# The second matmul of a score tile, 64 or 128 rows deep

## The chip, the cores and the metric

One core of a Trainium2 chip runs the whole program. The metric is the device time of one execution in microseconds; the time given is the median of three runs. The engines are named as the profile names them: PE (matmul; PEld is its weight load), DVE, ACT, POOL and SP, whose queue starts the DMAs.

## The reference

The program is an encoder trunk of two layers over 1024 tokens of width 1024, all in float32. Layer 0 mixes tokens by differential attention: 8 heads, each with two score maps of head dimension 64, a distance penalty and a softmax over all keys. Layer 1 mixes by a windowed attention of 16 heads of dimension 64 on a 16 x 64 grid. Both are followed by a gated feed-forward part (hidden width 2816) and a gated embedding that is added.

```python
s = jnp.einsum("mbhqd,mbhkd->mbhqk", qblk, k).astype(jnp.float32) * scale + bias
a = jax.nn.softmax(s, axis=-1)
a = a[0] - lam * a[1]
...
s = jnp.einsum('bhqd,bhkd->bhqk', qr, kb).astype(jnp.float32) + bias
s = jnp.where(key_mask, s, -jnp.inf)
a = jax.nn.softmax(s, axis=-1)
```

## The kernel before

Every float32 matrix is split into a high and a low part, and a product is made of the parts' products. For a score tile (128 queries x 512 keys in layer 0, x 384 or 256 in layer 1) the head dimension is only 64, so the query's two parts are stacked into one tile of 128 rows, `qs`: for map (or head) m = 0 the high part in rows 0 to 63 and the low part in rows 64 to 127, for m = 1 the other way round. The key's high part is stored twice, `kh`, in both halves of the rows: one 128-row product (L193) gives high x high plus low x high. The key's low part, `kl`, is stored once, m = 0 in the upper rows and m = 1 in the lower: a second product of 64 rows (L196) gives high x low. Both accumulate into one bank of PSUM, `s`.

`qk` makes these tiles for one head (layer 0) or one pair of heads (layer 1): per operand and half 24 products (L131) into a tile `d`, then ACT writes the high parts, DVE subtracts to get the low parts (L170, L173), and POOL copies the high part of the key to the other half (L185).

In layer 0, `attend` goes over eight blocks of 128 queries. For a block it scores 4 tiles (two maps, two halves of the keys), DVE adds the distance penalty and takes the running maximum (L273), ACT takes exponentials (L281), POOL scales one map and DVE subtracts the other (L298, L300), PE transposes the result (L306, 8 products a block), ACT and DVE split it into parts `at` (L89, L92), and 24 products with the values for each two blocks (L312) and a norm follow. Score tiles have three banks, exponentials four buffers, two a block. In heads 0 to 3 (`PAIRED`) the two maps of a key half are issued together, in the others one tile after another. In layer 1 the same steps run over 16 blocks (two heads of a pair, eight column blocks): score, bias and maximum (L421), exponential (L425), scaling on POOL (L428), transpose (L432), split, products with the values (L407).

While one head attends, PE also does the projections of the next heads: 96 products of `qk` (L131) for each head and 192 of `values` (L209) for each two heads, at the last head the first part of the output projection (L495). The program is written head after head; a scheduler puts it in order at build time, and each engine then follows its own fixed list. The projections are what it mixes between score tiles. How far ahead they can be placed depends on free buffers: `qs`, `kh` and `kl` have two each, the value tiles `v` four (`% 4`), each 8 KB a partition.

Of the kernel before, what the change touches and what calls it, by code (L numbers as in the profile page):

```python
# [12 lines left out]
F32 = mybir.dt.float32  # L13
F32R = mybir.dt.float32r
F16 = mybir.dt.float16
AF = mybir.ActivationFunctionType
ALU = mybir.AluOpType
# [3 lines left out]
P = 128  # L21
D = 1024
S = 1024
NT = S // P
# [17 lines left out]
MASKED = -1e30  # L42
RING = 5
EARLY = 5
# heads whose two maps are scored together, so that their 64-row products share the array
PAIRED = 4
EXP_LN_SET = 6
# the three products that carry a float32 product: (stationary part, moving part)
PASSES = ((0, 0), (0, 1), (1, 0))


class Trunk:
# [21 lines left out]
        self.hs = self.dram.tile([NT, P, D], F32, name="hs")  # L74
        self.hp = self.dram.tile([NT, P, D], F32, name="hp")

# [1 line left out]
    def open_hn(self):  # L78
        self.hnpool = self.tc.alloc_tile_pool(name=self.nc.get_next_instruction_name(), bufs=1, side="right",
                                              reuse_waits="tile")  # L80
# [58 lines left out]
                    self.nc.tensor.matmul(ps[:, c], lhs(i, k), rhs(j, k, c),  # L139
                                          start=k == 0 and n == 0, stop=k == nk - 1 and n == 2)  # L140

# [1 line left out]
    def qk(self, u, pools, bias=None, q_scale=1.0):  # L143
        nc = self.nc
        qkp, psd = pools["qk"], pools["d"]
        qs = qkp.tile([P, 2, S], F32R, tag=f"qs{u % 2}", name="qs")
        kh = qkp.tile([P, 2, S], F32R, tag=f"kh{u % 2}", name="kh")
        kl = qkp.tile([P, S], F32R, tag=f"kl{u % 2}", name="kl")
        top, bot = slice(0, 64), slice(64, 128)
        for which in range(2):  # L150
            w = self.weights(pools["wqk"][2 * u + which], self.slab, "slab")
            b = None if bias is None else bias[:, which * 8 + u:which * 8 + u + 1]
            for half in range(2):
                c = slice(half * HALF, (half + 1) * HALF)
                ps = psd.tile([P, HALF], F32, tag="d", name="d")
                self.mm_feat(ps, w, half)

                sc = q_scale if which == 0 else 1.0

                def hi(out, rows):  # L160
                    if b is None and sc == 1.0:
                        nc.scalar.copy(out=out, in_=ps[rows])
                    elif b is None:
                        nc.scalar.activation(out=out, in_=ps[rows], func=AF.Copy, scale=sc)
                    else:
                        nc.scalar.activation(out=out, in_=ps[rows], func=AF.Identity, bias=b[rows], scale=1.0)

                def lo(out, rows, h):
                    if b is None:
                        nc.vector.scalar_tensor_tensor(out=out, in0=ps[rows], scalar=sc, in1=h.bitcast(F32),  # L170
                                                       op0=ALU.mult, op1=ALU.subtract)
                    else:
                        nc.vector.scalar_tensor_tensor(out=out, in0=ps[rows], scalar=b[rows], in1=h.bitcast(F32),  # L173
                                                       op0=ALU.add, op1=ALU.subtract)

                if which == 0:
                    hi(qs[top, 0, c], top)
                    hi(qs[bot, 1, c], bot)
                    lo(qs[bot, 0, c], top, qs[top, 0, c])
                    lo(qs[top, 1, c], bot, qs[bot, 1, c])  # L180
                else:
                    hi(kh[top, 0, c], top)
                    hi(kh[bot, 1, c], bot)
                    for m, (to, src) in enumerate(((bot, top), (top, bot))):
                        nc.gpsimd.tensor_scalar(out=kh[to, m, c], in0=kh[src, m, c].bitcast(F32), scalar1=1.0,  # L185
                                                scalar2=0.0, op0=ALU.mult, op1=ALU.add)
                    lo(kl[top, c], top, kh[top, 0, c])
                    lo(kl[bot, c], bot, kh[bot, 1, c])
        return qs, kh, kl

    def score_part(self, part, s, qs, kh, kl, m, qc, kc):
        if part == 0:
            self.nc.tensor.matmul(s, qs[:, m, qc], kh[:, m, kc], start=True, stop=False)  # L193
        else:
            b = slice(64 * m, 64 * m + 64)
            self.nc.tensor.matmul(s, qs[b, m, qc], kl[b, kc], start=False, stop=True)  # L196

    def scores(self, *args):
        for part in range(2):
# [11 lines left out]
                                          start=k == 0 and n == 0, stop=k == KT - 1 and n == 2)  # L211
            sink(t, ps)

# [1 line left out]
    def diff_attention(self, first):  # L215
        nc, tc, a = self.nc, self.tc, self.a
        with ExitStack() as st:
            pool = lambda name, bufs, **k: st.enter_context(tc.tile_pool(name=name, bufs=bufs, reuse_waits="tile", **k))
            pools = {"qk": pool("da_qk", 1), "wqk": a["da_qk"]}
            vp = pool("da_v", 1)  # L220
# [24 lines left out]
            vt = {}  # L245

            def values(p2, psd):
                for j in range(2):
                    vt[2 * p2 + j] = vp.tile([P, NT, 2, P], F32R, tag=f"v{(2 * p2 + j) % 4}", name="v")

                def sink(t, ps):
                    for j in range(2):
                        v = vt[2 * p2 + j]
                        self.split((v[:, t, 0], v[:, t, 1]), ps[:, j * P:(j + 1) * P], nc.scalar)
                self.v_units(p2, a["da_v"], psd, sink, first if p2 == 0 else None)

            def attend(h, ops):
                qs, kh, kl = ops
                v = vt[h]
                otile = self.ob.tile([P, 2, CB, P], F32R, tag="ot", name="ot")  # L260
                ot = otile.rearrange("p l b (r c) -> p l b r c", c=8)
                for ch in range(4):
                    at = atp.tile([P, 2, NT, 256], F32R, tag="at", name="at")
                    for i in (2 * ch, 2 * ch + 1):
# [13 lines left out]
                        def exponent(m):  # L278
# [3 lines left out]
                                                 scale=SLOPES[h], accum_out=sm[:, m:m + 1])  # L282

                        qc = slice(i * P, (i + 1) * P)
                        order = (((0, 0), (1, 0)), ((0, 1), (1, 1))) if h < PAIRED else \
                            (((0, 0),), ((0, 1),), ((1, 0),), ((1, 1),))
                        for group in order:
                            ps = [ps_s.tile([P, HALF], F32, tag="s", name="s") for _ in group]
                            for part in range(2):
                                for (m, half), s in zip(group, ps):  # L290
                                    self.score_part(part, s, qs, kh, kl, m, qc, slice(half * HALF, (half + 1) * HALF))
                            for (m, half), s in zip(group, ps):
                                biased_max(m, half, s)
                                if half == 1:
                                    exponent(m)
# [55 lines left out]
                    ops = project(h + 1)  # L351
            self.out_proj_first(0, a["da_wo"], psd)

# [1 line left out]
    def neighborhood_attention(self):  # L355
        nc, tc, a = self.nc, self.tc, self.a
        with ExitStack() as st:
# [13 lines left out]

            def values(p4, psd):
                for j in range(2):
                    vt[2 * p4 + j] = vp.tile([P, NT, 2, 2, 64], F32R, tag=f"v{(2 * p4 + j) % 4}", name="v")

                def sink(t, ps):
                    for j in range(2):
                        v = vt[2 * p4 + j]
                        src = ps[:, j * P:(j + 1) * P].rearrange("p (m d) -> p m d", m=2)
                        self.split((v[:, t, :, 0], v[:, t, :, 1]), src, nc.scalar)  # L380
                self.v_units(p4, a["na_v"], psd, sink)
# [79 lines left out]
                    ops = self.qk(u + 1, pools, bq)  # L461
            self.out_proj_first(1, a["na_wo"], psd)

# [1 line left out]
    def keep(self, layer, u, ot):  # L465
        if u == PAIRS - 1:
            self.last = ot
# [171 lines left out]
        self.close_hn()  # L639


# [1 line left out]
def _units(w, n, width):  # L643
    k = w.shape[0]
    return w.reshape(k // P, P, n, width).transpose(2, 1, 0, 3)
# [64 lines left out]
```

## Time and profile before

| what | us |
|---|---|
| median of 3 runs (lowest, highest) | 3075.58 (3072.76, 3077.97) |
| span of the profiled execution | 3072.8 |
| PE busy | 3025.0 (98%) |
| PEld busy | 2410.6 (78%) |
| DVE busy | 1524.7 (50%) |
| ACT busy | 783.0 (25%) |
| POOL busy | 625.2 (20%) |

The profiled execution's time is the span, which is that of the fastest of the three runs to the tenth. Layer 0's attention lies between 71 and 740 us, layer 1's between 1695 and 2160 us of the span. A share over the whole span mixes stages: the feed-forward parts lie between and behind. Products are pipelined, so that the busy time of a product overlaps that of the next; how much time one adds is read from starts or from the chain of work that ended last.

### The profile page before, as it was taken

The numbers are of one execution on the slowest core, as the hardware profiler recorded it, in microseconds if no ns is written. First come the engines' busy times: TensorE is split into PE (matmuls) and PEld (weight loads), VectorE is DVE, ScalarE is ACT, GpSimd is POOL, SyncE is SP. The second block draws the span as 40 slices with busy tenths as digits, with TensorE's granted clock in tenths as the row PEclk, the third lists the DMA queues.
The fourth block names the chain that finished last, engine by engine and source line by source line (L and its number), as shares of the span: only waits on it lengthen the run. The fifth ranks groups of instructions, "written<-read, shape, count | busy, mean of one in ns | idle before, by whom it ended". The sixth has DMA issues, their size and how long they took to land.

```text
span 3072.8 us, 36422 instructions
## 1 busy us (share of the span) xinstructions
PE 3025.0 (98%) x14304; PEld 2410.6 (78%) x14304; DVE 1524.7 (50%) x2793; ACT 783.0 (25%) x1576; POOL 625.2 (20%) x766
## 2 busy tenths in 40 slices
PE   7999999999999999999999999999999999999998
PEld 7777777677788888888888878877778888888886
DVE  5677777775622323333444565666533333322354
ACT  3445454443200000000212444543200000000021
POOL 2232333332200000010112332332210001000121
PEclk9999999999999999999999999999999999999999
DMA  3010101243211111111123121136321111111112
GB/s 132 15 42 28 42 28 35 73 147 113 94 48 48 49 48 48 42 48 54 38 74 102 39 82 54 60 104 203 129 62 48 42 48 49 48 48 49 50 45 78
DMA packets 83866, 198.54 MB, mean 65 GB/s; under 512 B 6768, under 2 KB 39664, under 8 KB 83696
## 3 DMA queue, kind: packets, MB, share of 16 engines
q1 hardware_dynamic: 83696, 196.22, 20.4%
q8 instruction: 113, 1.85, 0.3%
q14 instruction: 57, 0.47, 0.1%
HBM read 164.74 MB, written 31.46 MB: 64 GB/s over the span
## 4 chain that ended last, share of the span: by engine, by line
PE 96%; DVE 2%; DMA 1%; issue 1%; ACT 0%; POOL 0%; POOLq 0%; SPq 0%; DVEq 0%; ACTq 0%
PE mm L131 32%; PE mm L139 17%; PE d L131 12%; PE d L209 7%; PE mm L599 6%; PE s L196 5%; PE d L495 3%; PE av L312 3%; PE s L193 3%; PE tr L306 2%; PE mm L595 1%; PE o L407 1%; PE tr L124 1%; PE tr L432 1%; DMA st<-da_wo 0%
## 5 line engine op out<-in xcount | busy, mean ns | idle before, releaser
L131 PE MATMUL mm<-hnT,w 128*128 128x512 f32 x4224 | 997.9, 397 | 2.5 <-DVE h L518 1.5
L131 PEld LDWEIGHTS mm<-hnT,w 128*128 128x128 f32 x4224 | 796.1, 189 | 197.5 <-POOL rs L113 1.7
L91 POOL TENSOR_SCALAR w<-st 128x1024 fp32r<-128x1024 f32 (+1 forms) x248 | 256.1, 1034 | 1619.2 <-PE mm L131 794.4
L92 DVE TENSOR_TENSOR w<-st,w 128x1024 fp32r<-128x1024 f32 (+1 forms) x248 | 282.8, 1142 | 490.1 <-POOL w L91 489.7
L139 PE MATMUL mm<-w,act 128*128 128x512 f32 x2112 | 486.0, 390 | 0.9 <-DVE h L552 0.9
L139 PEld LDWEIGHTS mm<-w,act 128*128 128x128 f32 x2112 | 395.7, 188 | 83.9 <-DVE h L552 1.7
L131 PE MATMUL d<-hnT,w 128*128 128x512 f32 x1536 | 405.0, 407 | 0.0
L131 PEld LDWEIGHTS d<-hnT,w 128*128 128x128 f32 x1536 | 280.1, 189 | 80.6 <-issue 22.2
L552 DVE TENSOR_TENSOR h<-h,mm 128x1024 f32<-128x1024 f32 x176 | 213.6, 1218 | 153.6 <-PE mm L139 153.2
L541 ACT ACTIVATE sil<-mm 128x1024 f32<-128x1024 f32 x44 | 45.4, 1031 | 791.4 <-PE mm L131 791.4
L542 DVE TENSOR_TENSOR sil<-sil,mm 128x1024 f32<-128x1024 f32 x44 | 53.7, 1221 | 374.1 <-PE mm L131 374.1
L209 PE MATMUL d<-w,hnT 128*128 128x256 f32 x1536 | 236.4, 295 | 1.6 <-POOL w L91 1.1
L209 PEld LDWEIGHTS d<-w,hnT 128*128 128x128 f32 x1536 | 201.2, 191 | 26.2 <-issue 21.8
L92 DVE TENSOR_TENSOR at<-tr,at 128x512 fp32r<-128x512 f32 (+2 forms) x288 | 157.4, 552 | 69.3 <-ACT at L89 56.0
L599 PE MATMUL mm<-w,hnT 128*128 128x512 f32 x768 | 188.4, 397 | 0.0
L281 ACT ACTIVATE e<-e,mx 128x1024 f32<-128x1024 f32 x128 | 147.2, 1150 | 130.9 <-DVE mx L279 126.1
L89 ACT CAST at<-tr 128x512 fp32r<-128x512 f32 (+2 forms) x288 | 133.6, 483 | 167.6 <-PE tr L432 106.2
L196 PE MATMUL s<-kl,qs 64*128 64x512 f32 (+2 forms) x384 | 175.5, 473 | 0.0
L89 ACT CAST act<-sil 128x1024 fp32r<-128x1024 f32 x44 | 46.4, 1054 | 489.6 <-DVE sil L542 489.6
L599 PEld LDWEIGHTS mm<-w,hnT 128*128 128x128 f32 x768 | 143.1, 188 | 33.5
L193 PE MATMUL s<-kh,qs 128*128 128x512 f32 (+2 forms) x384 | 156.7, 414 | 7.3 <-DVE kl L170 3.1
L196 PEld LDWEIGHTS s<-kl,qs 64*128 64x128 f32 x384 | 68.2, 183 | 93.5 <-issue 91.0
(101 smaller groups left out, 3003.0 us busy)
## 6 DMA issues: line engine op xcount, KB each, us to landing
st<-gu SPq DMA_DIRECT2D x88, 512.0 KB, 3.6
st<-wd SPq DMA_DIRECT2D x44, 512.0 KB, 3.5
ot<-ot SPq DMA_DIRECT2D x28, 512.0 KB, 3.9
o<-ot SPq DMA_DIRECT2D x16, 640.0 KB, 4.7
st<-da_qk SPq DMA_DIRECT2D x16, 512.0 KB, 3.6
hp<-r SPq DMA_DIRECT2D x16, 512.0 KB, 4.7
r<-hp SPq DMA_DIRECT2D x16, 512.0 KB, 3.5
st<-wpg SPq DMA_DIRECT2D x16, 512.0 KB, 3.6
```

Of the source, the lines that this page charges most:

```text
L89: hi_engine.copy(out=w[0], in_=src)
L91: hi_engine.tensor_scalar(out=w[0], in0=src, scalar1=1.0, scalar2=0.0, op0=ALU.mult, op1=ALU.add)
L92: self.nc.vector.tensor_tensor(out=w[1], in0=src, in1=w[0].bitcast(F32), op=ALU.subtract)
L131: self.nc.tensor.matmul(ps, w[:, i, kt * P:(kt + 1) * P], self.hnT[half][:, j, kt, :], start=kt == 0 and n == 0, stop=kt == KT - 1 and n == 2)
L139: self.nc.tensor.matmul(ps[:, c], lhs(i, k), rhs(j, k, c), start=k == 0 and n == 0, stop=k == nk - 1 and n == 2)
L193: self.nc.tensor.matmul(s, qs[:, m, qc], kh[:, m, kc], start=True, stop=False)
L196: self.nc.tensor.matmul(s, qs[b, m, qc], kl[b, kc], start=False, stop=True)
L209: self.nc.tensor.matmul(ps, self.hnT[t // 4][:, i, k, c], ws[k // 4][:, j, (k % 4) * 256:(k % 4 + 1) * 256], start=k == 0 and n == 0, stop ...
L281: nc.scalar.activation(out=e[m], in_=e[m], func=AF.Exp, bias=mx[:, m:m + 1], scale=SLOPES[h], accum_out=sm[:, m:m + 1])
L312: nc.tensor.matmul(av, v[:, kb, x], at[:, y, kb, :], start=kb == 0 and n == 0, stop=kb == NT - 1 and n == 2)
L552: nc.vector.tensor_tensor(out=h[t], in0=h[t], in1=acc, op=ALU.add)
L599: nc.tensor.matmul(acc[:, 0], self.hnT[t // 4][:, i, k, cs], ws[k // 2][:, j, k % 2], start=k == 0 and n == 0, stop=k == KT - 1 and n == 2)
```

## The change

The key's low part becomes a tile of the same shape as the high part. DVE writes it to the same rows as before, one plane for each m, and POOL copies each plane to the other half of the rows, as it does with the high part. The second product then takes all 128 rows of the stacked query and of the doubled low part; it adds low x low, which was left out before. The order of the score tiles is now one for all heads: the two key halves of a map together. Value tiles have three buffers in place of four.

```diff
-        kl = qkp.tile([P, S], F32R, tag=f"kl{u % 2}", name="kl")
+        kl = qkp.tile([P, 2, S], F32R, tag=f"kl{u % 2}", name="kl")
...
                     hi(kh[top, 0, c], top)
                     hi(kh[bot, 1, c], bot)
-                    for m, (to, src) in enumerate(((bot, top), (top, bot))):
-                        nc.gpsimd.tensor_scalar(out=kh[to, m, c], in0=kh[src, m, c].bitcast(F32), scalar1=1.0,
-                                                scalar2=0.0, op0=ALU.mult, op1=ALU.add)
-                    lo(kl[top, c], top, kh[top, 0, c])
-                    lo(kl[bot, c], bot, kh[bot, 1, c])
+                    lo(kl[top, 0, c], top, kh[top, 0, c])
+                    lo(kl[bot, 1, c], bot, kh[bot, 1, c])
+                    for x in (kh, kl):
+                        for m, (to, src) in enumerate(((bot, top), (top, bot))):
+                            nc.gpsimd.tensor_scalar(out=x[to, m, c], in0=x[src, m, c].bitcast(F32), scalar1=1.0,
+                                                    scalar2=0.0, op0=ALU.mult, op1=ALU.add)
...
     def score_part(self, part, s, qs, kh, kl, m, qc, kc):
-        if part == 0:
-            self.nc.tensor.matmul(s, qs[:, m, qc], kh[:, m, kc], start=True, stop=False)
-        else:
-            b = slice(64 * m, 64 * m + 64)
-            self.nc.tensor.matmul(s, qs[b, m, qc], kl[b, kc], start=False, stop=True)
+        self.nc.tensor.matmul(s, qs[:, m, qc], (kh, kl)[part][:, m, kc], start=part == 0, stop=part == 1)
...
-                    vt[2 * p2 + j] = vp.tile([P, NT, 2, P], F32R, tag=f"v{(2 * p2 + j) % 4}", name="v")
+                    vt[2 * p2 + j] = vp.tile([P, NT, 2, P], F32R, tag=f"v{(2 * p2 + j) % 3}", name="v")
...
-                        order = (((0, 0), (1, 0)), ((0, 1), (1, 1))) if h < PAIRED else \
-                            (((0, 0),), ((0, 1),), ((1, 0),), ((1, 1),))
-                        for group in order:
+                        for group in (((0, 0), (0, 1)), ((1, 0), (1, 1))):
...
-                    vt[2 * p4 + j] = vp.tile([P, NT, 2, 2, 64], F32R, tag=f"v{(2 * p4 + j) % 4}", name="v")
+                    vt[2 * p4 + j] = vp.tile([P, NT, 2, 2, 64], F32R, tag=f"v{(2 * p4 + j) % 3}", name="v")
```

On PE, in the middle of head 0 of layer 0, the order before has products of the next values (`d<-w,hnT`) between all score tiles:

```order
L209 MATMUL d<-w,hnT_96 128x256 x10
L193 MATMUL s<-kh,qs 128x512
L196 MATMUL s<-kl,qs 128x512
L209 MATMUL d<-w,hnT_96 128x256 x8
L312 MATMUL av<-at,v 128x256
L209 MATMUL d<-w,hnT_96 128x256
L193 MATMUL s<-kh,qs 128x512
L196 MATMUL s<-kl,qs 128x512
L209 MATMUL d<-w,hnT_96 128x256 x4
```

In the changed kernel the last of these stand in the middle of head 0, and score tiles, transposes (`tr`) and value products (`av`) follow alone (L191 is both products of a tile, L204 was L209, L299 was L306, L305 was L312):

```order
L204 MATMUL d<-w,hnT_95 128x256 x7
L191 MATMUL s<-kh,qs 128x512
L191 MATMUL s<-kl,qs 128x512
L299 MATMUL tr<-ident,e 128x128 x8
L191 MATMUL s<-kh,qs 128x512
L191 MATMUL s<-kl,qs 128x512
L191 MATMUL s<-kh,qs 128x512
L191 MATMUL s<-kl,qs 128x512
L191 MATMUL s<-kh,qs 128x512
L191 MATMUL s<-kl,qs 128x512
L305 MATMUL av<-at,v 128x256
```

The next product of a projection comes 23 tiles after the one at the top, 13 tiles into head 1: most value products of the next pair have moved from the first head into the second.

On PE, where head 2 of layer 0 begins in the changed kernel, the projection of its keys (L129, was L131) ends right ahead of its first score tile:

```order
L129 MATMUL d<-hnT_96,w 128x512
L299 MATMUL tr<-ident,e 128x128 x8
L312 MATMUL msp<-sq,ones 128x256
L129 MATMUL d<-hnT_96,w 128x512 x23
L191 MATMUL s<-kh,qs 128x512
L191 MATMUL s<-kl,qs 128x512
L305 MATMUL av<-at,v 128x256
L129 MATMUL d<-hnT_95,w 128x512 x2
L305 MATMUL av<-at,v 128x256 x23
L129 MATMUL d<-hnT_95,w 128x512 x4
L191 MATMUL s<-kh,qs 128x512 x2
L191 MATMUL s<-kl,qs 128x512
```

Before, the last product of that projection stood 18 rows ahead of the head's first score tile.

## Rows read from the trace of the kernel before

**Rows 1.** Windows: us, then busy us (instructions) per engine, granted clock, DMA.

```profile
core 0: us, PE busy (x) PEld busy (x) DVE busy (x) ACT busy (x) POOL busy (x), PEclk, DMA share, GB/s
...
149.20:234.70 85.50, 85.50 (x456) 64.89 (x454) 66.27 (x154) 41.70 (x87) 31.36 (x35) 1.00 0.12 38
...
1695.00:2092.00 397.00, 391.11 (x2092) 313.22 (x2091) 246.40 (x735) 187.43 (x486) 131.77 (x179) 1.00 0.24 74
```

**Rows 2.** The chain: start us, us it adds, what; plain products and transposes.

```profile
424.98 0.87 PE tr L306 x8
...
1672.77 22.49 PE d L131 x96
```

**Rows 3.** The chain around one score tile, and a run of value products.

```profile
228.83 0.23 PE s L193
229.06 0.42 PE s L196
229.49 1.84 PE d L131 x7
231.32 2.74 PE av L312 x23
```

**Rows 4.** Timeline of PE in head 0: start us, us, what.

```profile
117.02 0.50 PE L196 MATMUL s<-kl,qs 64*128 64x512 f32 x2
```

**Rows 5.** Timeline of PE in layer 1, two tiles running.

```profile
1795.27 0.44 PE L193 MATMUL s<-kh,qs 128*128 128x384 f32 x1
1795.64 0.44 PE L196 MATMUL s<-kl,qs 64*128 64x384 f32 x1
1796.01 4.24 PE L131 MATMUL d<-hnT,w 128*128 128x512 f32 x17
```

**Rows 6.** Groups of DVE, 71 to 740 us: busy us, mean ns, idle before.

```profile
L273 DVE CUSTOM_DVE_ANT_0 e<-s,strip,mx 128x512 f32<-128x512 f32 x128 | 95.1, 745 | 43.0 <-PE s L196 42.2
L273 DVE CUSTOM_DVE_ANT_0 e<-s,strip 128x512 f32<-128x512 f32 x128 | 87.5, 685 | 37.2 <-PE s L196 23.5 <-PE tr L306 12.4
L92 DVE TENSOR_TENSOR at<-tr,at 128x512 fp32r<-128x512 f32 x128 | 86.6, 684 | 10.4 <-ACT at L89 10.2
L300 DVE SCALAR_TENSOR_TENSOR e<-e,rc 128x1024 f32<-128x1024 f32 x64 | 85.4, 1335 | 11.8 <-POOL e L298 11.5
...
L273 DVE DVE_READ_ACCUMULATOR2_ANT mx<- 128x1 f32 x256 | 20.9, 82 | 0.0
...
L279 DVE TENSOR_SCALAR mx<-mx 128x1 f32<-128x1 f32 x128 | 18.3, 145 | 0.5
L330 DVE SCALAR_TENSOR_TENSOR o<-o,sub,y 128x256 f32<-128x256 f32 x30 | 18.1, 602 | 1.9 <-POOL y L329 1.8
L297 DVE TENSOR_TENSOR rc<-rc,neglam 128x1 f32<-128x1 f32 x64 | 16.0, 250 | 1.0
L92 DVE TENSOR_TENSOR ot<-o,ot 128x256 fp32r<-128x256 f32 x30 | 14.0, 466 | 0.7 <-ACT ot L89 0.4
...
L323 DVE TENSOR_SCALAR sq<-msp 128x256 f32<-128x256 f32 x31 | 13.0, 420 | 12.4 <-PE msp L319 12.2
...
L296 DVE RECIPROCAL rc<-sm 128x2 f32<-128x2 f32 x64 | 10.3, 161 | 18.9 <-ACT e L281 18.7
```

**Rows 7.** Windows around the late weights of the output projection, layer 0.

```profile
595.00:605.00 10.00, 7.53 (x31) 5.46 (x30) 6.38 (x14) 3.84 (x7) 4.85 (x4) 0.83 0.58 159
...
608.00:624.00 16.00, 13.18 (x56) 8.52 (x55) 15.55 (x33) 6.43 (x13) 6.47 (x7) 0.93 0.65 188
```

**Rows 8.** Groups of DVE, 1695 to 2092 us.

```profile
L421 DVE CUSTOM_DVE_ANT_0 s<-s,bias 128x384 f32<-128x384 f32 x84 | 47.1, 563 | 27.1 <-PE s L196 26.3
...
L92 DVE TENSOR_TENSOR at<-tr,at 128x384 fp32r<-128x384 f32 x55 | 30.2, 552 | 16.5 <-ACT at L89 16.1
...
L448 DVE SCALAR_TENSOR_TENSOR of<-o,bq,tmp 64x1024 f32<-64x1024 f32 x13 | 16.7, 1282 | 3.3 <-ACT tmp L447 3.1
...
L421 DVE DVE_READ_ACCUMULATOR2_ANT mx<- 128x1 f32 x112 | 15.2, 136 | 0.2
...
L92 DVE TENSOR_TENSOR ot<-of,ot 128x1024 fp32r<-128x1024 f32 x6 | 7.4, 1226 | 0.0
```

**Rows 9.** Copies of the key's high part, whole span.

```profile
L185 POOL TENSOR_SCALAR kh<-kh 64x512 fp32r<-64x512 f32 x64 | 51.5, 804 | 48.8 <-ACT kh L162 24.1 <-issue 10.6 <-ACT kh L166 9.5
```

More of the change, by code (lines that the diff above doesn't have):

```diff
@@ L44 @@
 EARLY = 5
-PAIRED = 4
 EXP_LN_SET = 6
```

## The prediction

> **What bounds the kernel now.** First the windows, one for the second head of layer 0 and one for nearly all of layer 1: PE has no gap in the first (85.50 of 85.50 us) and next to none in the second (391 of 397), while DVE works 66.27 us (0.78) and 246 us [rows 1]. Both attention layers are bound by PE, with DVE second and, in layer 0, not far behind. A busy PE may still stream little, so the next view is the chain in order of time, which counts only what each product adds: a run of 96 ordinary 512-column products takes 22.49 us, 0.234 us each [rows 2].
>
> In the chain around one score tile the full-depth product (L193) adds 0.23 us, the 64-row one (L196) 0.42, and the run of seven L131 behind it takes 1.84 us, where seven at 0.234 are 1.64 [rows 3]. So a 64-row product costs 0.19 us more than a full one of as many columns, and the product behind it another 0.20: **0.385 us a tile** over two plain products.
>
> **What the change removes.** All 384 second products become 128-row ones, priced at 0.234 us each since L131 has the same form [rows 2]. Layer 0 has 256 tiles. Where two 64-row products with different halves stand side by side they start within one piece of 0.50 us, x2 [rows 4]: there the second is free. This happens at 12 places in the whole trace, all in heads 0 to 3, so 24 tiles gain only 0.385 - 0.234 = 0.15 us a pair. Layer 0: 232 x 0.385 + 12 x 0.15 = 91 us. In layer 1 consecutive starts of L193, L196 and the next product are 0.37 us apart, 0.74 a tile [rows 5]; two plain 384-column products would be 2 x 0.234 x 384/512 = 0.35, so 0.385 again, and 128 tiles give 49 us. Together 140 us, if PE stays the only limit.
>
> A rule that speaks against the change: the Trainium skill, TensorEngine Tiling (Array Packing), Theoretical Speedup, says that products of at most 64 rows can run two at a time, up to twice as fast. The pair of [rows 4] agrees; if every tile had been so paired, layer 0 would gain 128 x 0.15 = 19 us, not 91. What is left here goes by the 12 places.
>
> **What it moves.** The low part of the key doubles in size, and the value tiles go from four buffers to three. A head pair then can't have both next value tiles while its first head still reads one. The order shows the consequence. Before, no more than five tiles stand between two pieces of projection work. Now the first head of a pair gets 96 projection products and 48 of the values', and then there is nothing to mix in until that head's last product with its values is done: 23, 26 and 25 tiles in a row in layer 0 (the last ten or so of heads 0, 2, 4 and the first half of the head behind), three times 12 in layer 1, with only their own transposes and value products.
>
> In such a stretch a block of 128 queries (4 tiles) needs of PE: 8 products x 0.234 = 1.9; 8 transposes 0.9 (0.87 in the chain [rows 2]); 12 value products at 2.74/23 = 0.12, 1.4 [rows 3]; 0.1 for the norm: 4.35 us. Of DVE it needs, from [rows 6]: four biased maxima 4 x 0.715 and their four readouts 0.33; the small ones 0.29, 0.16, 0.25; the combination 1.335; two splits of 0.684; half of 0.42 + 0.60 + 0.47, once in two blocks. That is 7.34 us. **DVE becomes the limit there.**
>
> How much of a stretch DVE can fill is not shown for a stretch like this. From 608 to 624 us, the place where weights of the output projection come late and PE works 13.18 us, it was 15.55 of 16, 0.97 [rows 7]; with PE never short it is 0.78 [rows 1]. I take 0.92, nearer to the first, where PE has gaps as here, and keep 0.85 and 0.97 as bounds.
>
> Layer 0: 74 tiles are 18.5 blocks, DVE 136 us, at 0.92 148 us, where PE needs 80: 68 us lost. The other stretches with few products a tile (16 tiles in head 0 beside 96 projection products; 21 tiles in head 5 beside 144 of values) come close to DVE too; 21 tiles are 38.5 us of DVE at 1.835 us each, 42 at 0.92, where PE needs 38. I put 13 us on all of these, an estimate, 0 to 20. Against it, DVE may still be behind when the next fill begins, and work that off later: three score banks are in flight, so some 3 us at each of three ends, -10.
>
> Layer 1: 12 tiles need of DVE 12 x (0.53 + 0.14 + 0.15 + 0.16) (0.56 for the wide tiles, less for the quarter with 256 columns), then 30 transposed blocks at 0.2 and 1.5 times 1.28 + 0.61 at the ends [rows 6, 8]: 20.8 us. PE needs 12 x 0.33 + 30 x 0.11 + 24 x 0.14 (value products by their widths) = 10.7. A tile passes five engines in turn here, so I take 0.90: 23.1 us, three times 12.4 us lost, less 1 us each of lag: 34.
>
> **The added copies.** POOL copies the low part as it copies the high one: 64 more, 0.80 us each in the mean [rows 9], 51 us. They wait for DVE's low part, so in POOL's queue whatever is behind them waits too: the next softmax scaling or weight split, by a microsecond or so. PE feels them where a second head of a pair ends: the last projection product now stands right ahead of the next head's first score, with 24 value products and 6 of the next projection, 4.3 us, as cover ahead of the second half of the keys. Four copies are 3.2 us, and the high part must first be made and the low part subtracted. Cover gone, 3.2 us at each head would be the price; I take 2 us at three heads of layer 0 and 1 us at three of layer 1: 6 and 3 us. DMAs and weights are as before.
>
> **The sum.** Layer 0: 91 - 68 - 13 + 10 - 6 = 14 us won. Layer 1: 49 - 34 - 3 = 12 us won. 3072.8 - 26 = 3046.8 for the profiled execution. Its span equals the lowest of three runs, with nothing shown around it; the median of the runs is 2.8 us higher, so **3049 us**. DVE's share alone gives 3036 us at 0.97 and 3065 at 0.85.
>
> **Rivals.**
> *The lag hides most of the stretches (faster).* If DVE holds 0.97 and carries a whole block (7.3 us) of lag over each end, layer 0 loses 140 - 80 - 22 + 3 = 41, layer 1 64 - 32 - 5 = 27: 91 + 49 - 68 = 72 us won, 3004 us. For it: in the order, 192 projection products come in the odd heads with only 19 or 11 tiles among them, room to catch up. Against it: only three score banks and two blocks' exponentials are held.
>
> *The clock falls in the stretches (slower).* PE would idle four tenths of each. In the windows with such idling the granted clock was 0.83 and 0.93 [rows 7]: part of each at 1.2 GHz, with PE busy 7.53 us of 10 and 13.18 of 16. At the low level a block costs PE 8.7 us, more than DVE's 8.0. If most of the stretches ran so, at 9.5 us a block: 18.5 x 1.5 = 28 us more in layer 0; in layer 1 21.4 us of PE in a chain with DVE, some 3 us each, 9; and some 10 for runs of fill that begin slow. 3049 + 47 = 3096 us. It turns the result to slower once about six tenths of the stretches run low. Against it: a slow PE idles less, so it may come back. The Trainium skill, TensorE: Matmul & The Clock Gate, A second HAM failure mode: psum-queue depth-cycling, tells of just such small idle times between groups that make the clock swing; by it the 3096 would be the time.
>
> *The copies hold up every head (slower).* If POOL's queue delays all 14 later heads by four copies, 14 x 3.2 = 45 us instead of 9: 3085 us. For it: POOL waits in order; against it: in the order only three starts a layer stand right behind the last projection product.
>
> *The change does not do what it says.* If the extra 0.385 us comes from something else than the 64 rows (two products that accumulate in one bank, or that load the same queries), it stays, and only the losses come: PE then needs 5.9 us a block, 148 - 109 = 39 and 3 x 7.7 = 23 us: about 3138. Against it: L131 accumulates in one bank too, at 0.234.
>
> **How the numbers follow.** The forecast with its own range, 3030 to 3068, has 0.50; the lag 0.17; the clock 0.20; the copies 0.08; no gain 0.05. A measurement of this kernel can tell about 0.2%, 6 us, from no change: below 3069.4 is faster, above 3081.7 slower. The forecast gives 0.45 to faster and 0.05 to within 0.2%; the lag 0.17 to faster; the clock, weak or strong, 0.03 to faster, 0.05 to within, 0.12 to slower; the copies 0.02 to within and 0.06 to slower; no gain 0.05 to slower. That makes 0.65, 0.12 and 0.23. The range, 3004 to 3093, leaves out the far half of the lag, the full clock case and no gain, some 2 in 10.
>
> **What would show it.** Second products spaced like first ones, and no 0.2 us behind them: 0.234 in the chain. In layer 0, three stretches of about 45 to 52 us in which PE is some 0.6 busy and waits for DVE's maxima, and DVE is 0.9 busy or more. The granted clock of these stretches decides between the forecast and the clock rival; POOL's L186 named by waiting score products, the copies. I am wrong if PE stays full there, or if DVE is well under 0.85 with PE waiting for something else.

## The result, and the profile after

| | median us (lowest, highest) | span of the profiled execution |
|---|---|---|
| before | 3075.66 (3072.76, 3077.97), 4 runs | 3072.8 |
| after | 3003.9 (3000.46, 3005.15), 4 runs | 3001.5 |

The change makes the kernel 72 us faster: 0.9765 of the time before, 95% interval 0.9751 to 0.9779. The forecast was 26 us faster, and its range, from 3004 on, just misses the measured time.

Between the first score of layer 0 and its last norm product lie 625.2 us, 672.5 before: 47 won, where 14 were forecast. Layer 1, from its first score to the first product of the stage behind its attention: 441.2 us against 464.9, 24 won, where 12 were forecast. The rest did not change.

From the page after: span, engines' busy time, and the chain's shares.

```profile
span 3001.5 us, 36482 instructions
...
PE 2917.3 (97%) x14304; PEld 2418.2 (81%) x14304; DVE 1528.3 (51%) x2793; ACT 777.1 (26%) x1576; POOL 668.3 (22%) x830
...
PE 91%; DVE 5%; issue 2%; POOL 1%; DMA 1%; ACT 1%; POOLq 0%; SPq 0%; DVEq 0%; ACTq 0%
```

PE lost 108 us of busy time, but only 71 us of span: it now has gaps. Windows of after (columns as in [rows 1]) show where: the three stretches without other work in layer 0, a window behind the first one with other work in it, two of layer 1's three stretches, and both stages whole.

```profile
120.80:158.90 38.10, 31.34 (x174) 23.29 (x173) 35.17 (x91) 24.25 (x50) 14.74 (x17) 0.96 0.00 1
271.30:312.80 41.50, 34.30 (x186) 24.57 (x185) 39.39 (x105) 26.59 (x54) 15.98 (x18) 0.96 0.00 1
419.80:461.40 41.60, 33.67 (x190) 25.62 (x188) 39.29 (x107) 27.50 (x57) 16.35 (x19) 0.96 0.00 1
...
158.90:184.00 25.10, 25.10 (x188) 23.93 (x187) 22.39 (x63) 15.17 (x36) 7.87 (x9) 1.00 0.14 43
...
1685.00:1703.00 18.00, 14.35 (x81) 10.57 (x79) 14.91 (x59) 13.47 (x39) 6.12 (x11) 1.00 0.08 26
1791.40:1810.10 18.70, 15.32 (x81) 11.90 (x79) 15.07 (x59) 13.54 (x39) 6.13 (x11) 0.91 0.08 25
...
71.60:696.80 625.20, 588.02 (x3344) 497.31 (x3343) 501.95 (x1201) 318.23 (x647) 243.17 (x274) 0.98 0.19 60
1649.00:2090.20 441.20, 424.44 (x2418) 366.99 (x2417) 282.94 (x842) 207.95 (x547) 164.86 (x228) 0.99 0.31 99
```

The stretches stand where the order showed them: 23, 26 and 25 tiles in layer 0, three times 12 in layer 1. PE is 0.80 to 0.83 busy there, DVE 0.92 to 0.95 in layer 0 and 0.81 to 0.83 in layer 1. With other work behind the first of them PE is full again. The stretches are shorter than forecast: 121.1 us in layer 0 (148 forecast), 55.0 in layer 1 (69.3).

The chain of after, where other work is at hand:

```profile
162.98 0.36 PE d L204 x3
163.34 0.46 PE s L191 x2
163.80 0.48 PE d L204 x4
```

A tile's two products take 0.46 us, 0.65 in [rows 3], and the four value projections behind add 0.12 each, like the three ahead: nothing is late behind the second product any more.

### The profile page after: what moved, and what is told of

It reads as the page before. It is cut to its first block, busy times and chain, and to the rows that moved or that the text cites. A ratio compares the mean times of both kernels' runs of the same rounds, so it can differ in the third digit from the quotient of the medians.

```text
span 3001.5 us, 36482 instructions
## 1 busy us (share of the span) xinstructions
PE 2917.3 (97%) x14304; PEld 2418.2 (81%) x14304; DVE 1528.3 (51%) x2793; ACT 777.1 (26%) x1576; POOL 668.3 (22%) x830
## 3 DMA queue, kind: packets, MB, share of 16 engines
q8 instruction: 113, 1.85, 0.3%
## 4 chain that ended last, share of the span: by engine, by line
PE 91%; DVE 5%; issue 2%; POOL 1%; DMA 1%; ACT 1%; POOLq 0%; SPq 0%; DVEq 0%; ACTq 0%
PE mm L129 33%; PE mm L137 18%; PE d L129 12%; PE d L204 6%; PE mm L592 6%; PE s L191 4%; PE d L488 3%; PE av L305 3%; PE mm L588 1%; PE tr L299 1%; PE tr L122 1%; PE o L400 1%; PE tr L425 1%; DVE e L268 1%; DVE at L90 1%
## 5 line engine op out<-in xcount | busy, mean ns | idle before, releaser
L129 PE MATMUL mm<-hnT,w 128*128 128x512 f32 x4224 | 997.7, 397 | 1.6 <-ACT hnT L87 0.5
L129 PEld LDWEIGHTS mm<-hnT,w 128*128 128x128 f32 x4224 | 795.5, 189 | 196.4 <-ACT hnT L87 1.0
L129 PE MATMUL d<-hnT,w 128*128 128x512 f32 x1536 | 386.3, 399 | 0.0
L129 PEld LDWEIGHTS d<-hnT,w 128*128 128x128 f32 x1536 | 286.6, 189 | 64.1
L204 PE MATMUL d<-w,hnT 128*128 128x256 f32 x1536 | 224.0, 290 | 2.0 <-POOL w L89 1.0
L204 PEld LDWEIGHTS d<-w,hnT 128*128 128x128 f32 x1536 | 207.0, 193 | 9.5 <-POOL w L89 1.4
L191 PE MATMUL s<-kh,qs 128*128 128x512 f32 (+2 forms) x384 | 154.2, 410 | 24.8 <-DVE mx L268 13.0
L191 PE MATMUL s<-kl,qs 128*128 128x512 f32 (+2 forms) x384 | 142.9, 379 | 0.0
L488 PE MATMUL d<-w,o 128*128 128x512 f32 x480 | 129.6, 406 | 7.4 <-POOL w L89 4.7
```

Source lines behind the costliest of these rows:

```text
L129: self.nc.tensor.matmul(ps, w[:, i, kt * P:(kt + 1) * P], self.hnT[half][:, j, kt, :], start=kt == 0 and n == 0, stop=kt == KT - 1 and n == 2)
L191: self.nc.tensor.matmul(s, qs[:, m, qc], (kh, kl)[part][:, m, kc], start=part == 0, stop=part == 1)
L204: self.nc.tensor.matmul(ps, self.hnT[t // 4][:, i, k, c], ws[k // 4][:, j, (k % 4) * 256:(k % 4 + 1) * 256], start=k == 0 and n == 0, stop ...
L488: nc.tensor.matmul(acc, o[:, k, i, :], ws[k][:, j, c], start=k == 0 and n == 0, stop=k == EARLY - 1 and n == 2)
```

## The experiments

Two theories were held against each other. **A**: the change takes 0.385 us a tile off PE, 140 us in all, and some 64 of them are given back in stretches where DVE limits, which come from the value buffers alone. **B**: only the 0.19 us in the second product itself was to be had, about 70 us, and the stretches cost nothing. Both give about 3000 to 3004 us for the changed kernel. Ratios are to the kernel before, timed again beside each run (3074.6 to 3075.2 us). e4 and e9 leave out low x low, as the kernel before does and with it e3, e6 and e8, which are made from it; the four whose names end in "twice" do some work again.

**e1_value_parts.** The changed kernel with value tiles in pieces, so that parts of both next tiles find room while the pair's first head still reads its own: halves in seven buffers in layer 0 (the room of 3.5 tiles), quarters in 13 in layer 1 (3.25 tiles). So the room grows too, from 3 tiles; pieces and room were not tried apart.

```diff
-                for j in range(2):
-                    vt[2 * p2 + j] = vp.tile([P, NT, 2, P], F32R, tag=f"v{(2 * p2 + j) % 3}", name="v")
+                for part in range(2):
+                    for j in range(2):
+                        n = 4 * p2 + 2 * part + j
+                        vt[2 * p2 + j, part] = vp.tile([P, NT // 2, 2, P], F32R, tag=f"v{n % 7}", name="v")
...
+                for u in (2 * p4 - 3, 2 * p4 - 2):
+                    free.extend(held.pop(u, []))
+                for part in range(4):
+                    for j in range(2):
+                        n = free.pop(0)
+                        held.setdefault(2 * p4 + j, []).append(n)
+                        vt[2 * p4 + j, part] = vp.tile([P, NT // 4, 2, 2, 64], F32R, tag=f"v{n}", name="v")
```

> The changed kernel with its value tiles cut into parts (halves in layer 0, seven buffers of 4 KB; quarters in layer 1, thirteen of 2 KB), so that three quarters (layer 0) and five eighths (layer 1) of the next pair's values can be made while the first head of a pair still reads its own; nothing else differs. Theory A (each second product of 64 rows cost 0.385 us on PE, 140 us in all, and about 64 us of that went back into the six stretches without other work, where DVE sets the time): the stretches vanish and most of the 64 us come, 3004 - 50 = about 2954 us (2940 to 2970). Rival B (the 72 us are the whole gain on PE, 0.19 us a tile, the excess of the 64-row product alone; what stands behind it in the chain is bookkeeping, and the stretches cost nothing net): 3004 us, within 6.

Measured: 2946.56 us, 0.9585 [0.957, 0.9599], 57 us less than after. Windows of this kernel: its head 1, then both stages.

```profile
139.70:207.70 68.00, 67.81 (x412) 59.69 (x411) 62.70 (x152) 39.63 (x84) 31.18 (x35) 1.00 0.13 40
72.20:656.80 584.60, 570.84 (x3344) 497.49 (x3343) 501.21 (x1201) 313.78 (x647) 250.13 (x274) 0.99 0.21 65
1610.10:2032.40 422.30, 413.12 (x2417) 363.60 (x2416) 280.45 (x842) 207.96 (x545) 164.97 (x228) 1.00 0.31 101
```

PE is full again (67.81 of 68.00), with DVE close behind (62.70). Layer 0 is 40.6 us shorter than after and layer 1 18.9. By B nothing was to be won here. This kernel is the fastest of this study, 128 us under the kernel before.

**e4_rows64.** The changed kernel, copies and buffers and all, but the second product on 64 rows again.

```diff
-        self.nc.tensor.matmul(s, qs[:, m, qc], (kh, kl)[part][:, m, kc], start=part == 0, stop=part == 1)
+        b = slice(64 * m, 64 * m + 64) if part else slice(0, P)
+        self.nc.tensor.matmul(s, qs[b, m, qc], (kh, kl)[part][b, m, kc], start=part == 0, stop=part == 1)
```

> The changed kernel with all its tiles, copies, buffers and order of tiles, but the second product takes 64 rows again (of the doubled low part only the half that was written first is read). A: 384 x 0.385 = 148 us more on PE, of which some 36 us hide in the stretches where DVE sets the time: 3004 + 105 = about 3109 us (3090 to 3125). B: 3004 + 72 = 3076 us.

Measured: 3112.77 us, 1.0125 [1.011, 1.014], 109 us more than after. That is more than B's whole 70, so the price is above 0.19 us a tile. Up to some 20 of the 109, an estimate from the stretches of layer 1 (see e3), go with a lower clock and not with the rows alone; e9 has the price without them.

**e3_before_three_values.** The kernel before with three value buffers.

```diff
-                    vt[2 * p2 + j] = vp.tile([P, NT, 2, P], F32R, tag=f"v{(2 * p2 + j) % 4}", name="v")
+                    vt[2 * p2 + j] = vp.tile([P, NT, 2, P], F32R, tag=f"v{(2 * p2 + j) % 3}", name="v")
```

(The same in layer 1.)

> The kernel before with three value buffers in place of four, and nothing else. A: in the stretches without other work PE then needs 5.9 us a block of queries (4.35 + 4 x 0.385), close to the 6.55 us that DVE gave in the changed kernel, so that little is lost: 18 blocks x 0.7 = 12 us in layer 0, 36 tiles x 0.22 = 8 us in layer 1, 3076 + 20 = 3096 us (3085 to 3110). B: the buffers cost nothing, 3076 us within 6.

Measured: 3114.98 us, 1.013 [1.0113, 1.0147]. The lost buffer alone costs 40 us, and e4 is level with this kernel: low part twice, its copies and the new tile order cost nothing that can be told. It is 19 us above what was expected, most of that in layer 1, which from its first to its last score takes 25 us longer (475 against 450; 8 were expected); layer 0 takes 15.5 longer (12 expected). Windows of a stretch of layer 0 and of two of layer 1:

```profile
125.70:161.50 35.80, 34.14 (x170) 22.42 (x169) 32.57 (x89) 22.40 (x46) 12.91 (x15) 1.00 0.00 1
1749.90:1775.10 25.20, 22.83 (x75) 15.31 (x74) 15.52 (x58) 13.87 (x38) 5.86 (x10) 0.61 0.05 19
1997.50:2019.70 22.20, 19.39 (x74) 13.11 (x73) 14.50 (x55) 13.14 (x36) 5.37 (x9) 0.77 0.06 21
```

In layer 0 this stretch needs 35.8 us for 22 tiles, 1.63 a tile, as after does with 1.64. The three together take 124.2 us for 72 tiles, 1.73 a tile (the second, 45.4 us for 25 tiles, at a granted clock of 0.85): in a stretch the 64 rows cost some 0.1 us a tile at most and not 0.385, since DVE needs about as long as PE. In layer 1 eleven tiles take 22 to 26 us at a granted clock of 0.59 to 0.77, where after's twelve took 18 to 19 at 0.91 to 1.00. e4's three there are like them (25.8, 22.1 and 22.9 us at 0.59, 0.77 and 0.74).

**e9_parts_rows64.** e1 with the second product on 64 rows, by the diff of e4.

> The kernel of e1 (value tiles in parts, no stretch without other work) with the second product back at 64 rows. It shows the price on PE where PE sets the time nearly everywhere. A: 384 x 0.385 = 148 us over e1's 2947, less some 10 to 15 us where DVE (0.9 busy in layer 0 in e1) would have set the time anyway: about 3082 us (3070 to 3100). B (0.19 us a tile): 2947 + 72 = 3019 us.

Measured: 3070.26 us, 0.9981 [0.9971, 0.999], 12 us better than expected and 124 more than e1. The two stages of this kernel, against e1's 584.60 and 422.30 us:

```profile
71.00:736.70 665.70, 657.41 (x3344) 486.75 (x3343) 502.87 (x1201) 318.91 (x647) 244.50 (x274) 0.99 0.19 57
1689.90:2155.20 465.30, 460.06 (x2418) 366.38 (x2417) 285.72 (x842) 210.25 (x546) 162.74 (x228) 0.99 0.28 92
```

81 and 43 us: where no such stretches stand, the 64 rows cost 0.32 us a tile (124 over 384 tiles). The chain of this kernel shows why it is under 0.385:

```profile
162.78 0.66 PE s L192 x2
163.44 0.59 PE tr L301 x4
...
165.27 2.37 PE s L192 x6
...
170.24 0.44 PE tr L301 x4
```

A tile takes 0.66 us (0.46 with 128 rows). The four transposes behind one take 0.59 us, where the four behind a value product take 0.44: 0.15 late, not 0.20. Three tiles in a row take 2.37, where 3 x 0.46 would be 1.38: 0.33 each.

**e2_value_halves_layer0.** e1's edit in layer 0 alone.

> As e1, in layer 0 alone; layer 1 keeps three whole value tiles. A: layer 0 lost 41 us in three stretches, some of it stays as DVE is the next limit: 3004 - 33 = 2971 us (2960 to 2985), and layer 1 as in the changed kernel, 441 us from its first score to its last. B: 3004 us.

Measured: 2962.06 us, 0.9634 [0.9619, 0.9648]. So 42 of the 57 us are layer 0's, close to the 41 that its three stretches lose against PE's 80 us.

**e5_dve_split_twice.** The changed kernel with DVE's half of the split done again.

```diff
                             self.split((at[:, 0, ks, c], at[:, 1, ks, c]), tr, nc.scalar)
+                            nc.vector.tensor_tensor(out=at[:, 1, ks, c], in0=tr, in1=at[:, 0, ks, c].bitcast(F32),
+                                                    op=ALU.subtract)
```

> The changed kernel in which DVE writes the low part of each split of layer 0 (at, 0.68 us, two a block of 128 queries) twice; 128 instructions more, 87 us by their durations, less by overlap. A: DVE sets the time in the stretches without other work, 18.5 blocks x 2 x 0.68 / 0.94 = 27 us there, and some 5 to 15 elsewhere since DVE comes near its limit: 3004 + 35 = about 3039 us (3025 to 3055). Rival (PE is the limit in the stretches too): at most 10 us, 3014 us.

Measured: 3032.02 us, 0.9856 [0.9841, 0.9871], 28 us more than after. The three stretches are 53.3, 52.5 and 44.4 us for 28, 28 and 25 tiles (74 in after), together 29 us longer: 1.85 a tile, so 0.87 us more in a block, in which two more splits of 0.60 (what one adds, below) stand. The first of them:

```profile
117.30:170.70 53.40, 42.86 (x204) 31.73 (x202) 47.86 (x122) 29.70 (x62) 15.35 (x19) 0.84 0.01 2
```

The stretches hold seven tiles more than in after, and these would have cost PE some 8 us elsewhere (4.35 us a block); so some 21 us are the stretches' own loss, and DVE's work counts there. Part of the first one may be its clock, 0.84 where after's was granted 0.96.

**e6_before_dve_split_twice.** The same in the kernel before, where PE limits, as a control.

> The same doubled instruction in the kernel before, as a control. A: PE sets the time throughout, and DVE's share of layer 0 goes from 0.75 to about 0.87, so little is lost: 3076 + 10 = 3086 us (3078 to 3095). If it costs as much here as in the changed kernel, the stretches are not what makes DVE the limit.

Measured: 3133.35 us, 1.0188 [1.0173, 1.0203], far from expected. The scheduler made another order, in which 18 and 20 tiles, among others, stand without other work. The first of these two stretches:

```profile
384.40:421.70 37.30, 31.89 (x133) 20.00 (x131) 32.92 (x82) 20.75 (x42) 12.95 (x17) 0.88 0.14 43
```

So it is no control; it only shows that such stretches can come without a lost buffer.

**e7_copies_twice.** The changed kernel with the low part copied twice.

```diff
-                    for x in (kh, kl):
+                    for x in (kh, kl, kl):
```

> The changed kernel in which POOL copies the key's low part twice: 64 copies more, 0.80 us each. A (the copies are hidden, POOL is 22% busy): 3004 to 3010 us. Rival (copies hold up the start of heads): 14 starts x 1.6 us = 22 us or more, 3026 us.

Measured: 2982.0 us, 0.9696 [0.968, 0.9712]: more work, and 22 us less than after. The order differs again: layer 0's stretches have 22, 23 and 23 tiles and take 110.6 us, 10.5 less; layer 1's have 11 each and take 50.7, 4.3 less. But nine tiles have left the stretches, and PE needs its time for them elsewhere (by the prediction's needs 1.09 and 0.89 us each, some 9 us), so shorter stretches explain only some 6 of the 22 us; where the rest comes from is open.

**e12_parts_copies_twice.** The same edit in e1.

> The kernel of e1 with the copies of the low part made twice, as in e7. Without stretches there is nothing that the doubled copies could shorten: if the gain of e7 came from shorter stretches, this stands at e1's 2947 us, or up to 10 us above for POOL's 51 us more. If doubled copies help by themselves, 2925 us.

Measured: 2948.42 us, 0.9586 [0.9572, 0.9601], level with e1: copying twice does not help by itself, and no cost of the copies shows in the sum. The order moved here too (layer 0 takes 590.5 us where e1 took 584.6, and the rest is some 4 us shorter). That e7's gain was one of order is the likely reading, not shown.

**e11_copy_order.** Each map's high and low parts copied together, not both high parts first.

```diff
-                    for x in (kh, kl):
-                        for m, (to, src) in enumerate(((bot, top), (top, bot))):
+                    for m, (to, src) in enumerate(((bot, top), (top, bot))):
+                        for x in (kh, kl):
```

> The changed kernel with POOL's four copies in another order: both of map 0 first, then both of map 1; the stretches keep their 23, 26, 25 and three times 12 tiles. In e7 twice as many copies made the kernel 22 us faster, with stretches of 22, 23, 23 and three times 11 tiles. If that came from the stretches (9 tiles fewer, at 1.5 to 1.7 us each) and the rest of the order, this kernel is at 3004 us within 6. If copies that end later or earlier are worth something by themselves, it moves by more.

Measured: 3003.43 us, 0.9763 [0.9747, 0.978]: no difference from after.

**e10_old_tile_order.** The changed kernel with the tile order of the kernel before.

```diff
-                        for group in (((0, 0), (0, 1)), ((1, 0), (1, 1))):
+                        for group in (((0, 0), (1, 0)), ((0, 1), (1, 1))) if h < 4 else \
+                            (((0, 0),), ((0, 1),), ((1, 0),), ((1, 1),)):
```

> The changed kernel with the tile order of before in layer 0 (the two maps of a key half together in heads 0 to 3, one tile after another in the rest). A: the order of tiles is no part of the gain; three stretches of 25, 26 and 23 tiles stay, 74 as in the changed kernel: 3004 us within 10. A rival in which the new order of tiles gives part of the gain: 3015 us or more.

Measured: 2999.41 us, 0.975 [0.9736, 0.9765]; the intervals overlap, so no gain from the new tile order can be told.

**e8_before_all_paired.** The kernel before with all eight heads issued in pairs.

```diff
-PAIRED = 4
+PAIRED = 8
```

> The kernel before with the two maps of a key half issued together in all eight heads of layer 0, not only in four. A: where two 64-row products with different halves stand side by side, 0.385 - 0.15 = 0.235 us are saved; before this happened at 12 places of the first four heads, so some 12 more make 3 us: 3073 us, no difference that can be told. If the scheduler kept all pairs together, 64 more places would give 15 us, 3061 us.

Measured: 3076.63 us, 1.0002 [0.9993, 1.0011]. Issued in pairs is not run in pairs: the timeline has 21 pieces like that of [rows 4] in place of 12. The order changed elsewhere too: the last head now ends with 12 tiles without other work. The Trainium skill (TensorEngine Tiling (Array Packing), Theoretical Speedup) gives up to twice the speed for products of at most 64 rows; the pairs agree (two products in 0.50 us, [rows 4]), but 21 pairs for 256 tiles are too few to show it in the time, and no run has all of them paired.

## Why the prediction was wrong

Times of the four combinations, and the kernel before beside them:

| value tiles | 64 rows | 128 rows | difference |
|---|---|---|---|
| three whole | 3113 (e4) | 3004 (after) | 109 |
| in pieces | 3070 (e9) | 2947 (e1) | 124 |
| four whole | 3076 (before) | not tried | |

Theory A is borne out: 3076 becomes 3115 by the lost buffer (e3), stays at 3113 with copies and tile order (e4), falls to 3004 with 128 rows, and to 2947 once the stretches have work in them (e1). The 109 us hold what e4 loses by a lower clock in layer 1. Four whole value tiles with 128 rows were not tried; the doubled low part takes 8 KB a partition more (two buffers of 4 KB), the size of one value tile.

**PE's price nearly held.** e1, which has no such stretches, takes 584.60 and 422.30 us for the two layers, the kernel before 672.5 and 464.9: 88 and 43 us won, of 91 and 49 forecast. e9 and e1, in the new tile order, give 0.32 us a tile and not 0.385, because less than 0.20 comes behind the product there. In after, layer 0's 47 us won and the 41 that the stretches lose (121 against PE's 80) make 88; layer 1's 24 and 23 (55.0 against PE's 32) make 47. Outside the stretches little was lost: PE's gaps there, in layer 0, are 15.3 us (37.2 in the stage less 21.9 in the three), and 11.3 in the window of the kernel before that stands below (669.00 less 657.69).

**The stretches of layer 0 held**: their places, their tiles, DVE's share (0.92 taken, 0.92 to 0.95 measured), and what PE waits for. That PE is 0.81 to 0.83 busy there, and not some 0.6, goes with the view, which counts a product's whole duration and not only what it adds. Waits of after, 120.8 to 158.9 us:

```profile
PEld s L191 <- DVE mx L268: 8.5, 12, 2.0
PE s L191 <- DVE mx L268: 4.8, 6, 1.5
```

**In layer 1 the places and tiles held, the limit did not.** DVE is 0.81 to 0.83 busy where 0.90 was taken, and PE's score products wait for ACT's exponential (L418), which reads the score bank last, not for DVE's maximum. Waits of after, 1685 to 1703 us:

```profile
PEld s L191 <- ACT e L418: 3.8, 7, 1.4
PE s L191 <- ACT e L418: 2.0, 4, 1.2
```

So there it is the chain through five engines that sets the time; that DVE alone does is not shown.

**The step that failed is DVE's need in a block, "That is 7.34 us".** It added mean durations, and DVE's instructions overlap. In the view of [rows 6] this can be read from the kernel before: its 16 groups (11 of them shown there) sum to 563.4 us, but this window, of the kernel before, shows DVE's busy time:

```profile
71.00:740.00 669.00, 657.69 (x3328) 487.12 (x3327) 496.79 (x1199) 319.94 (x644) 221.15 (x243) 0.99 0.19 56
```

That is 0.88 of the sum. In after's first stretch the groups of DVE (busy us, mean ns, idle before) are these, and six smaller ones of 6.3 us in all:

```profile
L293 DVE SCALAR_TENSOR_TENSOR e<-e,rc 128x1024 f32<-128x1024 f32 x6 | 8.1, 1358 | 1.1 <-POOL e L291 1.1
L268 DVE CUSTOM_DVE_ANT_0 e<-s,strip,mx 128x512 f32<-128x512 f32 x11 | 8.1, 740 | 0.1
L268 DVE CUSTOM_DVE_ANT_0 e<-s,strip 128x512 f32<-128x512 f32 x10 | 6.8, 683 | 0.4 <-PE tr L299 0.4
L90 DVE TENSOR_TENSOR at<-tr,at 128x512 fp32r<-128x512 f32 x10 | 6.5, 677 | 0.0
L290 DVE TENSOR_TENSOR rc<-rc,neglam 128x1 f32<-128x1 f32 x6 | 3.8, 627 | 0.0
...
L268 DVE DVE_READ_ACCUMULATOR2_ANT mx<- 128x1 f32 x21 | 1.7, 79 | 0.0
```

Together 41 us, against 35.17 of busy time. The chain of after in that stretch, which counts what each one adds, shows by how much:

```profile
132.88 0.39 DVE o L323
133.27 0.60 DVE e L268
133.87 0.01 DVE mx L268
133.88 0.66 DVE e L268
...
134.55 0.60 DVE at L90
135.15 0.33 DVE ot L90
...
136.76 0.06 DVE mx L274
```

A maximum behind other work of DVE adds 0.60 to 0.66 us where the sum had 0.715, its readout 0.01 where it had 0.08, a split 0.60 for 0.684, a small one 0.06 for 0.145. The combination (L293) is the exception: 1.19 to 1.60 in the chains of the three stretches, with 1.335 in the sum. Over the whole stage of after, DVE is busy for 501.95 us. The weights, key and query parts, values and output projection (w, kl, qs, v and r in the view of [rows 6], not among the rows shown there) are 98 us by durations, 86 at 0.88; the other 416 over 64 blocks are 6.5 us a block. That takes one ratio for all of DVE's work, an estimate. With 6.5 the forecast's own step gives 18.5 x 6.5 / 0.92 = 131 us for the stretches and not 148. The stretches held 113.9 us of DVE's busy time, 6 less than 18.5 x 6.5, so that much, it seems, was worked off behind them; 131 less 6 / 0.92 is 124, near the measured 121.

**The same error stood in two more terms.** The other stretches with few products (13 us) priced 21 tiles at 1.835 us of DVE each; at 6.5 / 4 = 1.63 they need 37 us, no more than PE's 38, and should cost nothing, which the small gaps outside the three stretches bear out. Layer 1 was given 20.8 us of DVE for 12 tiles; the groups in its first stretch sum to 18.9 us, and DVE is busy for 14.91. Its loss was 23 us and not 34; this term explains it in part only, since DVE alone does not set the time there. Of the 45 us between forecast and time, the stretches make 28 (41 lost where 68 less 10 of lag were forecast, and 23 for 34); most of the other 17 are these 13 us and the copies' 9, of which little was found.

**The copies.** Forecast 9 us in all; e12, with each low part copied twice, is 2 us above e1. The waits of after name POOL's copies ahead of a score product in layer 0 once:

```profile
PEld s L191 <- POOL kh L186: 3.2, 1, 3.2
...
PE s L191 <- POOL kh L186: 2.8, 1, 2.8
```

**The rivals.** The lag gave 3004 us, and 3004 came, but not by its mechanism: it wanted DVE at 0.97 and 22 us carried over the ends in layer 0; DVE was at 0.92 to 0.95 and about 6 us were carried. Two wrong numbers made its sum right. The clock rival did not come about in after, where the stretches were granted 0.91 to 1.00; with 64 rows, in layer 1 of e3 and e4, it did, at 0.59 to 0.77. The Trainium skill (TensorE: Matmul & The Clock Gate, A second HAM failure mode: psum-queue depth-cycling) tells of a clock that swings with small idle times between groups of products; after's dips are such a swing, but far short of the price that the prediction put on it. That PE's price comes from elsewhere than the 64 rows is refuted by e4 and e9, whose programs change the rows alone.

One reading in the sum looks about 1 us off: the profiled span was taken for the fastest run's time, and 2.8 us added for the median. In the changed kernel the profiled execution took 3003.46 us where its span is 3001.5, only 2.0 less.

## What to carry to other kernels

Price every engine that may become the limit by what its instructions add (the chain, the busy time of a window, the distance of starts), not by the sum of their durations; the sum of all groups beside the busy time of the same window shows at once how far the two differ. Ask which buffers pay for a change, and what can then no longer be mixed in: here one value buffer cost 40 us by itself, part of it by a lower clock, and value tiles in pieces, with half a tile more room in layer 0 and a quarter in layer 1, brought back 57 with the 128 rows. Where a scheduler makes the order, a small edit can move 20 us or more in either direction (e6, e7), so a control must be looked at for its order before its time says anything.

## What was not expected of the hardware

In layer 1 the stretches of e3 and e4 fell to the lower clock. Windows of e3 in the first of them:

```profile
1730.00:1750.00 20.00, 20.00 (x121) 17.09 (x120) 10.91 (x36) 8.93 (x25) 7.71 (x12) 1.00 0.15 50
1750.00:1753.00 3.00, 2.61 (x13) 1.49 (x11) 2.23 (x7) 1.89 (x4) 0.00 (x0) 1.00 0.01 3
1753.00:1757.00 4.00, 3.25 (x13) 2.26 (x13) 2.92 (x16) 2.11 (x7) 1.29 (x3) 0.82 0.00 0
1757.00:1761.00 4.00, 4.00 (x15) 3.00 (x13) 2.16 (x10) 1.48 (x5) 1.06 (x2) 0.50 0.30 108
1761.00:1765.00 4.00, 4.00 (x15) 2.86 (x13) 1.52 (x6) 1.93 (x7) 1.87 (x3) 0.50 0.02 6
1765.00:1769.00 4.00, 3.92 (x13) 2.71 (x12) 1.91 (x8) 2.17 (x7) 1.15 (x2) 0.50 0.00 0
1769.00:1775.00 6.00, 4.86 (x12) 2.81 (x13) 4.58 (x14) 4.19 (x10) 0.40 (x1) 0.50 0.00 0
```

PE was full until 1750, then 5.86 of 7 us busy, and the clock fell to 0.50 (1.2 GHz). It stayed there to the end of the stretch, though PE was busy 11.92 of the 12 us from 1757 (then 4.86 of 6): a slow PE that idles less did not bring the clock back here, as the prediction had thought it might. Three of the six stretches of e3 and e4 are like this one (0.59 to 0.61 in the mean); the other three, at 0.74 to 0.77, were at the higher level for more of their time. After's stretch from 1791.4 us also dips, and recovers sooner:

```profile
1796.00:1800.00 4.00, 3.99 (x19) 3.44 (x18) 3.28 (x15) 2.21 (x7) 2.21 (x4) 0.62 0.00 0
1800.00:1805.00 5.00, 4.82 (x30) 3.94 (x28) 4.14 (x21) 3.90 (x14) 2.30 (x4) 0.96 0.31 93
```

Why the 64-row kernels stay low for longer than the 128-row one is open; no run here separates the rows from the number of products in a stretch.
